# Seven products of quarters for the attention's values, in one stage behind the first gates

## The chip, the cores and the metric

The kernel runs on one core of a Trainium2 chip. The metric is the time of one execution on the device in microseconds (us); three executions of the kernel before gave a median of 658.37 us (658.17 to 658.61).

## The reference, cut to what matters

One layer of a hybrid encoder over 512 tokens of width 1024. A normed input `h` is projected once into ten groups of 1024 columns; two branches (attention with 8 heads of 128, retention with 4 heads of 256) are gated, projected and merged:

```
h = rms_norm(x, norm_gain)
sb_q, sb_k, sb_v, sb_g, r_q, r_k, r_v, r_g, m_sb, m_ret = split(h @ w_in)
z   = q.k / sqrt(128)                  # per head, 512 x 512, only s < t
w   = sigmoid(z) * prod_{s<j<t} (1 - sigmoid(z_j))
out_a = (w @ v) * silu(sb_g)
out_b = rms_norm(retention(r_q, r_k, r_v)) * silu(r_g)
merged = sigmoid(m_sb + b0) * (out_a @ w_a) + sigmoid(m_ret + b1) * (out_b @ w_b)
out = x + merged @ w_o
```

The change concerns `sb_v`, a product of 512x1024 by 1024x1024.

## The kernel before, in words

Every fp32 product is made of three matmuls of rounded parts (`mm3`: hi by hi, hi by lo, lo by hi). A weight block is loaded by SyncE (SP), rounded to `hi` by ScalarE (ACT) and its rest `lo` is taken by VectorE (DVE); that pair is `split`, line 131 its DVE half. A *stage* (`dense`) makes 512 columns: for eight row blocks k and four output blocks j it issues three matmuls, 96 in all. It holds four of five PSUM banks. The stages in order: `qk0`, `v0`, `sg0`, `qk1`, `qk2`, `v1`, `sg1`, `qk3`, `ma0`, `rqk0`, `pa0`, `ma1`, `pa1`, `rg0`, `rv`, and then the retention's and the last ones. `qk` makes queries and keys of two heads, `v` and `sg` values and gates of four heads, `ma` merge gates, `rqk` the retention's queries and keys, `pa` the attention's output projection.

The stage `rv` is of another kind: it makes the 1024 columns of the retention's values at once, by seven products of 256 tokens by 512 rows by 512 columns (Strassen) in place of eight (`v_groups`, `strassen`, `quarter_sums`). Its weights come as quarters (`w_rv`), and four sums of the tokens' quarters (`s1`, `s2`, `s3`, `n4`) are made ahead of it on GpSimd (POOL) and split (`token_sums`, `made_sums`).

Small work runs beside the stages: generators in a list (`Interleaver`), of which the first is resumed at each `work.step()`, after each second j of a row block, so sixteen times a stage. The instructions of a generator thus stand on TensorE (PE) between six matmuls of the stage and the next six. Side work is: the transposes of queries and keys (`post` in `qk_group`, which waits `W_QK` = 8 steps and makes `pqk`), the row copies of the norm (`token_norm_rows`: `rc` on DVE, `pr` on PE), and `attention` for two heads: `z` (scores), then `beta` (two sigmoids on ACT, on DVE the mask's add, a scan, a product), `pw` (transposes of beta on PE, then split into `wT`), `po` (weights by values), and `oa` (`po` by gates, split). Its order is one `z` block, then `pw` of two blocks earlier, and `po` when a head is done. TensorE's order is that of the code. Where a result is needed that the side list has not yet made, `drain` resumes the list with no stage's matmuls between: `pa0` does so at row block k for `oa[k]`, since row block k is head k:

```
    def branch_act(parts):
        def act(k):
            work.drain(lambda: k in parts)
            return parts[k]
```

The other engines' order is set by a scheduler that knows priorities (`tc.high_priority` around the weights' splits) and its own estimates; SP's loads stay in the order of the code.

Of the kernel before, what the change touches and what calls it, by code (L numbers as in the profile page):

```python
# [7 lines left out]
F32 = mybir.dt.float32  # L8
# [5 lines left out]
S = 512  # L14
# [55 lines left out]


@with_exitstack
def hybrid_block(ctx, tc, x, x_t, vecs, w_in, w_rv, w_a, w_b, w_o, cos_t, sin_t, decay, out):
    nc = tc.nc
    PSUM = bass.MemoryType.PSUM

# [28 lines left out]
    def T_tile(name, dtype=F32R):  # L105
        return big.tile([P, 4, S], dtype, tag="T", bufs=4, name=name)
# [54 lines left out]
    def first_loads():  # L161

        raws = [wpool.tile([P, 2, S], F32, tag="raw", bufs=RAW_BUFS, name=f"first_raw{k}") for k in range(2)]
        xt = [T_tile(f"xt{hf}", F32) for hf in range(2)]
        for k in range(NK):
            ks = slice(k * P, (k + 1) * P)
            if k < 4:
                load_weights(raws[k // 2][:, k % 2 : k % 2 + 1, :], w_in, k, 1, ((C_Q, 256), (C_K, 256)))
            load(xt[k // 4][:, k % 4, :], x_t[ks, :])
        for k in range(NK):  # L170
            r = xt[k // 4][:, k % 4, :]
            g = vec[:, V_NG + k : V_NG + k + 1]
            for c in range(0, S, S // 2 if k == 0 else S):
                cs = slice(c, c + (S // 2 if k == 0 else S))
                nc.scalar.activation(xT_hi[:, k, cs], r[:, cs], AF.Copy, scale=g)  # L175
            nc.vector.scalar_tensor_tensor(  # L176
                xT_lo[:, k, :], r, g, f32(xT_hi[:, k, :]), op0=ALU.mult, op1=ALU.subtract
            )
        return raws

    first = first_loads()

    idle = tmp.tile([P, 2 * S], mybir.dt.bfloat16, tag="tmp", name="idle")[:, :S]
    nc.vector.memset(idle, 0.0)
# [70 lines left out]
    def proj(name, blocks, rows):  # L255
        return dense(name, lambda k: (xT_hi[:, k, :], xT_lo[:, k, :]), w_in, blocks, rows)
# [5 lines left out]
    sr = const.tile([P, S], F32, name="sr")  # L262

    def token_norm():
        yield 9
        ssx = small.tile([P, NT], F32, tag="ssx", bufs=1, name="ssx")
        ts = []
        for hf in range(2):
            t = T_tile(f"x{hf}", F32).rearrange("p a s -> p (a s)").rearrange("p (b d) -> p b d", b=2)
            ts.append(t)  # L270
            load(t, x[2 * hf * P : (2 * hf + 2) * P, :].rearrange("(b p) d -> p b d", p=P))
        for hf, t in enumerate(ts):
            for j in range(2):
                tb = 2 * hf + j
                s2 = small.tile([P, 2], F32, tag="s2", name="s2")
                sq = tmp_tile("sqx")
                for c in range(2):
                    nc.scalar.activation(sq, t[:, j, c * S : (c + 1) * S], AF.Square, accum_out=s2[:, c : c + 1])
                nc.vector.tensor_add(ssx[:, tb : tb + 1], s2[:, 0:1], s2[:, 1:2])
        rsqrt(rx, ssx, D, NT)  # L280
        nc.gpsimd.tensor_mul(rx2, rx, rx)
        yield 1

    def token_norm_rows():

        load(cr, cos_t)
        load(sr, sin_t)
        yield 5
        pr = side_psum("pr")
        for tb in range(NT):  # L290
            rc = tmp_tile("rc")[:, :P]
            nc.vector.tensor_copy(rc, rx[:, tb : tb + 1].broadcast_to([P, P]))
            matmul(pr[:, tb * P : (tb + 1) * P], rc, ident, start=True, stop=True)
        nc.vector.tensor_copy(rb, pr)
        nc.gpsimd.tensor_mul(cr, cr, rb)
        nc.gpsimd.tensor_mul(sr, sr, rb)
        yield 1
# [3 lines left out]
    def qk_group(p):  # L301

        ps = proj(f"qk{p}", ((C_Q + 256 * p, 256), (C_K + 256 * p, 256)), True)
        ss = small.tile([P, NT, 4], F32, tag="ss", name=f"ss{p}")
        raws = []
        for tb in range(NT):
            raw = tmp.tile([P, 4, P], F32, tag="qraw", bufs=4, name=f"qraw{p}_{tb}")
            nc.scalar.copy(raw, ps[tb].rearrange("p (h d) -> p h d", h=4))
            raws.append(raw)
        for tb in range(NT):  # L310
            sq = tmp_tile("sqq").rearrange("p (h d) -> p h d", h=4)
            nc.scalar.activation(sq, raws[tb], AF.Square)
            nc.vector.reduce_sum(ss[:, tb, :], sq, axis=mybir.AxisListType.X)
        rr = small.tile([P, NT, 4], F32, tag="rr", name=f"rr{p}")
        nc.vector.tensor_mul(ss, ss, rx2.rearrange("p (b o) -> p b o", o=1).broadcast_to([P, NT, 4]))
        rsqrt(rr.rearrange("p b h -> p (b h)"), ss.rearrange("p b h -> p (b h)"), HD, 16)
        nc.gpsimd.tensor_mul(rr, rr, rx.rearrange("p (b o) -> p b o", o=1).broadcast_to([P, NT, 4]))
        for tb in range(NT):
            nc.gpsimd.tensor_tensor(
                raws[tb], raws[tb],  # L320
                rr[:, tb, :].rearrange("p (h o) -> p h o", o=1).broadcast_to([P, 4, P]), op=ALU.mult,
            )

        def post():
            hi, lo = T_tile(f"qk_hi{p}"), T_tile(f"qk_lo{p}")
            yield W_QK
            for tb in range(NT):
                pt = side_psum(f"pqk{p}_{tb}").rearrange("p (h d) -> p h d", h=4)
                for j in range(4):
                    transpose(pt[:, j, :], raws[tb][:, j, :], ident)  # L330
                ts = slice(tb * P, (tb + 1) * P)
                for c, a in ((V_QG, 0), (V_KG, 2)):
                    g = vec[:, c : c + 1]
                    nc.scalar.activation(hi[:, a : a + 2, ts], pt[:, a : a + 2, :], AF.Copy, scale=g)
                    nc.vector.scalar_tensor_tensor(
                        lo[:, a : a + 2, ts], pt[:, a : a + 2, :], g, f32(hi[:, a : a + 2, ts]),
                        op0=ALU.mult, op1=ALU.subtract,
                    )
# [7 lines left out]
    def v_group(name, c0):

        ps = proj(name, ((c0, S),), True)
        hi, lo = V_tile(f"{name}_hi"), V_tile(f"{name}_lo")
        for sb in range(NT):  # L350
            v_rows(hi, lo, sb, ps[sb])
        return [(hi[:, sb, :], lo[:, sb, :]) for sb in range(NT)]

    def v_rows(hi, lo, sb, src):
        r = rx[:, sb : sb + 1]
# [16 lines left out]
        split(hi, lo, t)  # L372
        sums[name] = (hi, lo)

    def token_sums(ready):

        xt = [V_tile(f"xs{hf}", F32) for hf in range(2)]
        for hf in range(2):
            load(xt[hf], x_t[4 * hf * P : 4 * (hf + 1) * P, :].rearrange("(k p) t -> p k t", p=P))
        yield 4  # L380
        for hf in range(2):
            for k in range(4):
                r = xt[hf][:, k, :]
                nc.scalar.activation(r, r, AF.Copy, scale=vec[:, V_NG + 4 * hf + k : V_NG + 4 * hf + k + 1])
                yield 1
        (x11, x21), (x12, x22) = halves(xt[0]), halves(xt[1])
        nc.gpsimd.tensor_sub(x22, x21, x22)
        nc.gpsimd.tensor_sub(x21, x11, x21)
        yield 1
        while not ready():  # L390
            yield 1
        made_sums("s1", x22)
        nc.gpsimd.tensor_sub(x22, x22, x11)
        yield 3
        made_sums("s3", x21)
        yield 3
        made_sums("s2", x22)
        nc.gpsimd.tensor_add(x12, x12, x22)
        yield 3
        made_sums("n4", x12)  # L400
        yield 1

    def quarter_sums(name, w, room):

# [82 lines left out]
        i, j = int(a[1]) - 1, int(a[2]) - 1  # L487
        return [t[:, 4 * j : 4 * j + 4, i * H : (i + 1) * H] for t in (xT_hi, xT_lo)]

    def v_groups(name, w):  # L490
        hi, lo = [V_tile(f"{name}0_hi")], [V_tile(f"{name}0_lo")]
        kept = {}

# [19 lines left out]
                elif n == 2:  # L513
                    v_rows(hi[0], lo[0], j, kept[1, j])

        room = [t(f"{name}_w{n}", F32) for n, t in enumerate((T_tile, V_tile, V_tile, T_tile))]
        strassen(name, w, room, put)
        hi.append(V_tile(f"{name}1_hi"))
        lo.append(V_tile(f"{name}1_lo"))
        for n in (3, 5):  # L520
# [187 lines left out]

    work.add(token_norm())
    qk_group(0)  # L710
    work.add(attention((0, 1), lambda: 0 in sg, lambda: v[0], lambda: sg[0]))
    v[0] = v_group("v0", C_V)
    sg[0] = silu_group("sg0", C_G)
    qk_group(1)
    work.add(attention((2, 3), lambda: 0 in sg, lambda: v[0], lambda: sg[0]))
    qk_group(2)
    work.add(attention((4, 5), lambda: 1 in sg, lambda: v[1], lambda: sg[1]))
    v[1] = v_group("v1", C_V + S)
    sg[1] = silu_group("sg1", C_G + S)
    qk_group(3)  # L720
    work.add(attention((6, 7), lambda: 1 in sg, lambda: v[1], lambda: sg[1]))
# [6 lines left out]
    for g in range(2):  # L728
        m = gate_group(f"ma{g}", C_MA + S * g, V_BM + 4 * g)
        if g == 0:  # L730
            ret(0, lambda: 5 in oa)
        else:
            work.side.insert(0, token_sums(lambda: len(pa) == 2))
            work.wait = 0
        ps = dense(f"pa{g}", branch_act(oa), w_a, ((S * g, S),), False)
        t = T_tile(f"pa{g}", F32)
# [114 lines left out]
```

## Time and profile before

| | before |
|---|---|
| median of three executions | 658.37 us |
| profiled execution, its own time | 658.81 us |
| its span (first to last instruction) | 657.0 us |
| TensorE busy | 650.5 us, 3073 matmuls |
| VectorE, ScalarE, GpSimd busy | 393.7, 276.2, 65.6 us |
| granted TensorE clock | full in all 40 slices |

The span is what the instructions cover; 1.8 us of the execution's own time lie around it. Matmuls are pipelined, so a matmul's shown duration (0.39 us for 512 columns) is longer than the distance from one to the next.

### The profile page before, as it was taken

The page shows a single profiled execution, that of the slowest core. Times are in us where ns is not written, and L with a number is a line of the kernel's source. Part 1 is how long each engine was busy: PE and PEld are TensorE (multiplying, and loading weights), DVE is VectorE, ACT ScalarE, POOL GpSimd, SP SyncE. Part 2 cuts the span into 40 slices and gives each one's busy share as a digit, 9 for nine tenths or more (in the row PEclk, how much of TensorE's full clock was granted, in tenths as well). Part 3 has the DMA queues.
Part 4 walks back from the last instruction along what each step waited for, and adds up shares of the span by engine and source line. Part 5 has one row for each costly group of instructions (what it writes and reads, how often), then busy time and mean ns, then how long its engine had stood idle before and what let it go on. Part 6 is the DMA issues. An engine that isn't in the chain of part 4 may idle for free.

```text
span 657.0 us, 7987 instructions
## 1 busy us (share of the span) xinstructions
PE 650.5 (99%) x3073; PEld 539.7 (82%) x3073; DVE 393.7 (60%) x582; ACT 276.2 (42%) x439; POOL 65.6 (10%) x58
## 2 busy tenths in 40 slices
PE   9999999999999999999999999999999999999997
PEld 6788888888888888888888878888888888888885
DVE  6356863596497477664464876386673862554632
ACT  5744534564364564332733554333342442422310
POOL 0051001250000400000330100200100101000000
PEclk9999999999999999999999999999999999999999
DMA  8543223322322312332538522232322322225441
GB/s 280 202 128 96 65 64 97 97 64 66 97 64 65 97 64 65 103 95 89 210 97 299 126 55 65 81 96 65 108 69 81 97 64 82 81 97 165 156 157 64
DMA packets 42503, 69.22 MB, mean 105 GB/s; under 512 B 2913, under 2 KB 19553, under 8 KB 42209
## 3 DMA queue, kind: packets, MB, share of 16 engines
q1 hardware_dynamic: 41168, 65.55, 31.4%
q0 software_dynamic: 576, 2.10, 1.7%
q10 hardware_dynamic: 720, 1.07, 0.4%
q8 instruction: 24, 0.39, 0.3%
q14 instruction: 15, 0.11, 0.1%
HBM read 65.55 MB, written 2.10 MB: 103 GB/s over the span
## 4 chain that ended last, share of the span: by engine, by line
PE 94%; DMA 3%; DVE 1%; ACT 1%; SPq 0%; issue 0%; DVEq 0%; ACTq 0%
PE rqk_ps L91 13%; PE qk_ps L91 10%; PE v_ps L91 7%; PE sg_ps L91 7%; PE pa_ps L91 7%; PE mb_ps L91 7%; PE ma_ps L91 7%; PE rg_ps L91 7%; PE fin_ps L91 7%; PE pb_ps L91 7%; PE rv_y L91 3%; PE rv_p L91 2%; PE po L91 2%; PE z L91 2%; PE rz L91 2%; PE ro L91 2%
## 5 line engine op out<-in xcount | busy, mean ns | idle before, releaser
L91 PE MATMUL rqk_ps<-xT_hi,rqk_hi 128*128 128x512 f32 x128 | 50.9, 397 | 0.0
L91 PE MATMUL qk_ps<-qk_hi,xT_hi 128*128 128x512 f32 x128 | 50.5, 402 | 0.0
L91 PE MATMUL rqk_ps<-xT_hi,rqk_lo 128*128 128x512 f32 x128 | 50.0, 391 | 0.0
L91 PE MATMUL rqk_ps<-xT_lo,rqk_hi 128*128 128x512 f32 x128 | 50.0, 391 | 0.0
L91 PE MATMUL qk_ps<-qk_hi,xT_lo 128*128 128x512 f32 x128 | 49.2, 392 | 0.2 <-DVE xT_lo L176 0.2
L91 PE MATMUL qk_ps<-qk_lo,xT_hi 128*128 128x512 f32 x128 | 49.0, 390 | 0.0
L91 PE MATMUL pa_ps<-oa,pa_hi 128*128 128x512 f32 x128 | 39.6, 390 | 0.0
L91 PE MATMUL pb_ps<-ob,pb_hi 128*128 128x512 f32 x128 | 39.4, 389 | 0.0
L569 DVE TENSOR_TENSOR_SCAN beta<-beta,zero 128x128 f32<-128x128 f32 (+3 forms) x32 | 26.9, 840 | 7.5 <-ACT beta L567 7.5
L91 PEld LDWEIGHTS qk_ps<-qk_hi,xT_lo 128*128 128x128 f32 x128 | 23.9, 188 | 5.8 <-DVE xT_lo L176 0.6
L91 PEld LDWEIGHTS rqk_ps<-xT_hi,rqk_lo 128*128 128x128 f32 x128 | 24.0, 188 | 5.2
L91 PEld LDWEIGHTS pa_ps<-oa,pa_hi 128*128 128x128 f32 x128 | 23.9, 188 | 5.3 <-ACT rk L620 0.4
L91 PEld LDWEIGHTS qk_ps<-qk_hi,xT_hi 128*128 128x128 f32 x128 | 24.0, 188 | 5.2 <-ACT xT_hi L175 0.8
L91 PEld LDWEIGHTS pb_ps<-ob,pb_hi 128*128 128x128 f32 x128 | 24.0, 188 | 5.0
L91 PEld LDWEIGHTS rqk_ps<-xT_hi,rqk_hi 128*128 128x128 f32 x128 | 24.1, 188 | 4.4
L91 PEld LDWEIGHTS rqk_ps<-xT_lo,rqk_hi 128*128 128x128 f32 x128 | 24.1, 188 | 4.2
L91 PEld LDWEIGHTS qk_ps<-qk_lo,xT_hi 128*128 128x128 f32 x128 | 24.1, 188 | 4.1
L205 POOL TENSOR_TENSOR rr<-ms,m_half 128x16 f32<-128x16 f32 x4 | 11.7, 2913 | 150.7 <-DVE ms L204 150.7
L91 PE MATMUL v_ps<-v_hi,xT_hi 128*128 128x512 f32 x64 | 26.1, 408 | 0.0
L131 DVE TENSOR_TENSOR qk_lo<-qk_raw,qk_hi 128x1024 fp32r<-128x1024 f32 x14 | 17.1, 1223 | 14.9 <-ACT qk_hi L130 14.9
L567 ACT ACTIVATE beta<-z 128x128 f32<-128x128 f32 (+3 forms) x32 | 14.0, 436 | 28.5 <-DVE z L564 28.2
L91 PE MATMUL sg_ps<-xT_hi,sg_hi 128*128 128x512 f32 x64 | 25.8, 404 | 0.0
(255 smaller groups left out, 1738.4 us busy)
## 6 DMA issues: line engine op xcount, KB each, us to landing
rqk_raw<-in_w_in SPq DMA_DIRECT2D x32, 256.0 KB, 3.0
qk_raw<-in_w_in SPq DMA_DIRECT2D x28, 256.0 KB, 3.0
v_raw<-in_w_in SPq DMA_DIRECT2D x8, 512.0 KB, 3.8
sg_raw<-in_w_in SPq DMA_DIRECT2D x8, 512.0 KB, 3.6
ma_raw<-in_w_in SPq DMA_DIRECT2D x8, 512.0 KB, 3.6
pa_raw<-in_w_a SPq DMA_DIRECT2D x8, 512.0 KB, 4.0
rg_raw<-in_w_in SPq DMA_DIRECT2D x8, 512.0 KB, 3.7
mb_raw<-in_w_in SPq DMA_DIRECT2D x8, 512.0 KB, 3.6
```

The source lines that it names most:

```text
L91: tc.keep_in_program_order(nc.tensor.matmul(*a, **k))
L131: nc.vector.tensor_sub(lo, src, f32(hi))
L205: nc.gpsimd.tensor_tensor(dst, t[:, :width], m_half[:, :width], op=ALU.pow)
L567: nc.scalar.activation(keep[:, :n], z[:, :n], AF.Sigmoid, scale=-sc)
L569: nc.vector.tensor_tensor_scan(keep[:, :n][:, ::-1], keep[:, :n][:, ::-1], zero.broadcast_to([P, n]), 1.0, op0=ALU.mult, op1=ALU.add,)
```

## The change

`sb_v` is now made as `rv` is, by seven products, in one stage `v` for both groups of heads; the stages `v0` and `v1` go. It stands behind `sg0`, and all four rounds of `attention` are added behind it. The tokens' sums for it are made from the first loads of x (kept in `first_xt`, scaled in place by eight `tensor_scalar_mul` on DVE, line 270 of the change), and `token_sums`, `token_norm_rows` and `post(0)` are side work of `sg0`, in this order. The norm's own loads of x go to V tiles. The diff, cut to its core:

```
+    def token_norm():
-        yield 9
+        yield 5
+        for hf in range(2):
+            yield 1
+            for k in range(4):
+                r = first_xt[hf][:, k, :]
+                nc.vector.tensor_scalar_mul(r, r, vec[:, V_NG + 4 * hf + k : V_NG + 4 * hf + k + 1])
+        yield 1
+        first_sums(first_xt)
+        yield 1
...
-            yield W_QK
+            yield W_QK if p else 1
...
+        if p == 0:
+            work.add(token_sums(first_xt))
+            work.add(token_norm_rows())
         work.add(post())
-        if p == 0:
-            work.add(token_norm_rows())
...
+    def first_sums(xt):
+        (x11, x21), (x12, x22) = halves(xt[0]), halves(xt[1])
+        nc.gpsimd.tensor_sub(x22, x21, x22)
+        nc.gpsimd.tensor_sub(x21, x11, x21)
+    def token_sums(xt, gap=2):
+        (x11, x21), (x12, x22) = halves(xt[0]), halves(xt[1])
+        made_sums("s1", x22)
+        nc.gpsimd.tensor_sub(x22, x22, x11)
+        yield gap
+        made_sums("s3", x21)
+        yield gap
+        made_sums("s2", x22)
+        nc.gpsimd.tensor_add(x12, x12, x22)
+        yield gap
+        made_sums("n4", x12)
+        yield 1
...
     work.add(token_norm())
     qk_group(0)
+    sg[0] = silu_group("sg0", C_G)
+    work.drain(lambda: "n4" in sums and 0 in qk_parts)
+    v[0], v[1] = v_groups("v", w_v, (V_tile, V_tile, T_tile, T_tile))
     work.add(attention((0, 1), lambda: 0 in sg, lambda: v[0], lambda: sg[0]))
-    v[0] = v_group("v0", C_V)
-    sg[0] = silu_group("sg0", C_G)
     qk_group(1)
     work.add(attention((2, 3), lambda: 0 in sg, lambda: v[0], lambda: sg[0]))
     qk_group(2)
     work.add(attention((4, 5), lambda: 1 in sg, lambda: v[1], lambda: sg[1]))
-    v[1] = v_group("v1", C_V + S)
     sg[1] = silu_group("sg1", C_G + S)
     qk_group(3)
     work.add(attention((6, 7), lambda: 1 in sg, lambda: v[1], lambda: sg[1]))
```

Where the change moves instructions is seen in the order of three places. First TensorE at the end of the last attention round (head 7: `z7_3` the scores' last block, `pw7_1` to `pw7_3` the transposes, `po7` weights by values). Before it stands in the stage `rqk0`, and six matmuls of that stage lie at each "...":

```order
L91 MATMUL z7_3_2360<-qk_hi3_1997,qk_lo3_1998 128x512
...
L94 MATMUL pw7_1_2376<-ident_131,beta7_1_2279 128x128 x2
...
L94 MATMUL pw7_2_2394<-ident_131,beta7_2_2308 128x128 x3
...
L94 MATMUL pw7_3_2406<-ident_131,beta7_3_2365 128x128 x4
...
L91 MATMUL po7_2419<-wT_0_76,v1_hi_1470 128x512
L91 MATMUL po7_2419<-wT_1_77,v1_hi_1470 128x512
```

In the change it stands in the stage `pa0`, the rows following one another with nothing between, except at "...", where the rest of `po7` is left out; the last row shown is the first matmul of row block 7:

```order
L91 MATMUL z7_3_2591<-qk_hi3_2200,qk_lo3_2201 128x512
L94 MATMUL pw7_1_2601<-ident_131,beta7_1_2511 128x128 x2
L94 MATMUL pw7_2_2606<-ident_131,beta7_2_2540 128x128 x3
L94 MATMUL pw7_3_2612<-ident_131,beta7_3_2596 128x128 x4
L91 MATMUL po7_2619<-wT_0_76,v1_hi_842 128x512
L91 MATMUL po7_2619<-wT_1_77,v1_hi_842 128x512
...
L91 MATMUL pa0_ps0_2365<-oa7_2634,pa0_hi6_2571 128x512 x2
```

The tail of head 7 has moved from `rqk0`, with stage matmuls in each gap, to the end of `pa0`, with none. Likewise `po6` stands directly ahead of the matmuls of row block 6, which read `oa6`.

Second, VectorE where the last attention round begins (`z6_0` its first block's masking, `beta6_0` the scan and product behind it). Before, that is at the end of `ma0` (`qk_lo3` are the transposed queries and keys):

```order
L131 TENSOR_TENSOR rqk0_lo0_2193<-rqk0_raw0_2189,rqk0_hi0_2192 128x1024
L335 SCALAR_TENSOR_TENSOR qk_lo3_1998<-pqk3_3_2104,vec_81,qk_hi3_1997 128x2x128
L564 TENSOR_TENSOR z6_0_2125<-z6_0_2125,neg_mask_136 128x128
L335 SCALAR_TENSOR_TENSOR qk_lo3_1998<-pqk3_3_2104,vec_81,qk_hi3_1997 128x2x128
L569 SCALAR_TENSOR_TENSOR beta6_0_2130<-beta6_0_2130,zero_78 128x128
L564 TENSOR_TENSOR z6_1_2141<-z6_1_2141,neg_mask_136 128x128
L573 TENSOR_TENSOR beta6_0_2130<-beta6_0_2130 128x127
```

In the change it is at the start of `pa0` (`rm`, `rk`, `rqk_lo0`: the rotation of the retention's first queries and keys, 16 instructions of 512 columns, of which the last six are shown):

```order
L636 TENSOR_TENSOR rm0_1_1_2352<-rk0_1_2334,sr_149 128x512
L637 TENSOR_TENSOR rm0_1_3_2354<-rk0_1_2334,cr_148 128x512
L131 TENSOR_TENSOR pa0_lo4_2497<-pa0_raw4_2494,pa0_hi4_2496 128x1024
L638 TENSOR_TENSOR rm0_1_0_2351<-rm0_1_0_2351,rm0_1_1_2352 128x512
L639 TENSOR_TENSOR rm0_1_2_2353<-rm0_1_2_2353,rm0_1_3_2354 128x512
L574 TENSOR_TENSOR z6_0_2381<-z6_0_2381,neg_mask_136 128x128
L131 TENSOR_TENSOR rqk_lo0_2332<-rm0_1_0_2351,rqk_hi0_2331 128x512
L131 TENSOR_TENSOR rqk_lo0_2332<-rm0_1_2_2353,rqk_hi0_2331 128x512
L579 SCALAR_TENSOR_TENSOR beta6_0_2386<-beta6_0_2386,zero_78 128x128
L574 TENSOR_TENSOR z6_1_2397<-z6_1_2397,neg_mask_136 128x128
L583 TENSOR_TENSOR beta6_0_2386<-beta6_0_2386 128x127
```

The masking and the scan of head 6 have moved behind the rotation and behind the split of `pa0`'s third weight block. On TensorE `z6_0` now stands behind the first six matmuls of `pa0`, and `pw6_0`, which reads `beta6_0`, behind its first 24 and `z6_0` to `z6_2`.

Third, VectorE where the row copies `rc` stand (`ss0`: the sums for the norm of queries and keys). Before, they are four in a row with small ones between, ahead of `v0`'s splits:

```order
L292 COPY rc_539<-rx_145 128x128
L315 TENSOR_TENSOR ss0_305<-ss0_305,rx2_146 128x16
L292 COPY rc_542<-rx_145 128x128
L204 TENSOR_SCALAR ms_328<-ss0_305 128x16
L292 COPY rc_545<-rx_145 128x128
L292 COPY rc_548<-rx_145 128x128
```

In the change three splits of token sums (`s3`, `s2`, `n4`), one of `sg0`'s weights, and the first split (`v_blo1`) and sum of the values' quarters stand between them:

```order
L300 COPY rc_443<-rx_145 128x128
L323 TENSOR_TENSOR ss0_315<-ss0_315,rx2_146 128x16
L131 TENSOR_TENSOR s3_lo_380<-xt0_88,s3_hi_379 128x1024
L204 TENSOR_SCALAR ms_338<-ss0_315 128x16
L131 TENSOR_TENSOR s2_lo_402<-xt1_89,s2_hi_401 128x1024
L131 TENSOR_TENSOR sg0_lo4_433<-sg0_raw4_430,sg0_hi4_432 128x1024
L131 TENSOR_TENSOR n4_lo_419<-xt1_89,n4_hi_418 128x1024
L131 TENSOR_TENSOR v_blo1_579<-v_w0_566,v_bhi1_578 128x1024
L300 COPY rc_446<-rx_145 128x128
L443 TENSOR_TENSOR v_w0_566<-v_w0_566,v_w1_567 128x1024
L300 COPY rc_449<-rx_145 128x128
L300 COPY rc_452<-rx_145 128x128
```

The last `rc`, which `pr` on TensorE reads, has moved behind work on the quarters' first loads. `pr` stands on TensorE behind the first 54 matmuls of `sg0` (before: behind its first 18).

## Rows read from the trace of the kernel before

**Rows 1.** The page's busy times of the engines.
```profile
PE 650.5 (99%) x3073; PEld 539.7 (82%) x3073; DVE 393.7 (60%) x582; ACT 276.2 (42%) x439; POOL 65.6 (10%) x58
```

**Rows 2.** Waits of TensorE: us in total, times, longest; the only one after 30 us.
```profile
PE rv_y L91 <- DVE rv_c L509: 0.7, 2, 0.4
```

**Rows 3.** The chain of waits: start us, us, what; its last stage, `rv`, `pr`.
```profile
55.98 0.89 PE pr L91 x8
...
365.62 5.44 PE rv_y L91 x24
...
404.95 1.37 PE rqk_ps L91 x6
...
609.30 43.53 PE fin_ps L91 x192
```

**Rows 4.** Groups of instructions: one of the three groups of the stages v0, v1.
```profile
L91 PE MATMUL v_ps<-v_hi,xT_hi 128*128 128x512 f32 x64 | 26.1, 408 | 0.0
```

**Rows 5.** Timeline of VectorE, start of the kernel: start us, us, engine, line, operation.
```profile
9.63 0.42 DVE L220 CAST qk_hi<-first_raw 128x512 fp32r<-128x512 f32 x1
9.97 0.74 DVE L176 SCALAR_TENSOR_TENSOR xT_lo<-xt,vec,xT_hi 128x512 fp32r<-128x512 f32 x1
...
11.23 3.39 DVE L176 SCALAR_TENSOR_TENSOR xT_lo<-xt,vec,xT_hi 128x512 fp32r<-128x512 f32 x5
15.35 1.23 DVE L131 TENSOR_TENSOR qk_lo<-qk_raw,qk_hi 128x1024 fp32r<-128x1024 f32 x1 [0.73 <-ACT qk_hi L130]
```

**Rows 6.** Timeline of TensorE, start of the kernel and the third weight block.
```profile
1.20 3.92 PE L91 MATMUL pi<-idle 128*128 128x512 bf16 x9 [1.20 <-DVE idle L184]
...
16.87 0.39 PE L91 MATMUL qk_ps<-qk_lo,xT_hi 128*128 128x512 f32 x1
```

**Rows 7.** Timeline of VectorE and GpSimd: first row copy, rx, a token sum.
```profile
33.35 0.22 DVE L292 COPY rc<-rx 128x128 f32<-128x128 f32 x1
...
28.54 1.03 POOL L205 TENSOR_TENSOR rx<-ms,m_half 128x4 f32<-128x4 f32 x1 [26.74 <-DVE ms L204]
...
323.98 3.27 POOL L388 TENSOR_TENSOR xs<-xs 128x1024 f32<-128x1024 f32 x1
```

**Rows 8.** Timeline of the DMA queue and ScalarE: rv's quarters, issue and first use.
```profile
347.35 2.90 SPq L134 DMA_DIRECT2D rv_w<-in_w_rv x6
...
352.13 1.05 ACT L130 CAST rv_bhi<-rv_w 128x1024 fp32r<-128x1024 f32 x1 [1.96 <-DMA rv_w<-in_w_rv]
```

**Rows 9.** VectorE around the first rotation: busy by stretch, and its timeline.
```profile
273.60:287.50 13.90, 13.90 (x62) 11.18 (x61) 13.20 (x20) 6.93 (x10) 0.00 (x0) 1.00 0.26 77
...
273.61 0.68 DVE L624 TENSOR_TENSOR rm<-rqk_ps,cr 128x512 f32<-128x512 f32 x1
274.21 0.68 DVE L625 TENSOR_TENSOR rm<-rqk_ps,sr 128x512 f32<-128x512 f32 x1
```

**Rows 10.** Timeline of head 7's last blocks on TensorE, VectorE, ScalarE; below, oa0.
```profile
264.02 0.39 PE L91 MATMUL z<-qk_hi,qk_lo 128*128 128x512 f32 x1
264.44 0.30 DVE L564 TENSOR_TENSOR z<-z,neg_mask 128x128 f32<-128x128 f32 x1 [1.27 <-PE z L91]
265.47 1.23 DVE L569 TENSOR_TENSOR_SCAN beta<-beta,zero 128x512 f32<-128x512 f32 x1 [0.72 <-ACT beta L567]
266.80 0.69 DVE L573 TENSOR_TENSOR beta<-beta 128x511 f32<-128x511 f32 x1
268.94 0.60 PE L94 MATMUL pw<-ident,beta 128*128 128x128 f32 x4
269.63 0.59 ACT L130 CAST wT<-pw 128x512 fp32r<-128x512 f32 x1 [1.35 <-PE pw L94]
270.25 0.69 DVE L131 TENSOR_TENSOR wT<-pw,wT 128x512 fp32r<-128x512 f32 x1 [0.82 <-ACT wT L130]
...
84.38 0.68 DVE L595 TENSOR_TENSOR oa<-po,sg 128x512 f32<-128x512 f32 x1
85.75 0.69 DVE L131 TENSOR_TENSOR oa<-oa,oa 128x512 fp32r<-128x512 f32 x1 [0.49 <-ACT oa L130]
```

More of the change, by code (lines that the diff above doesn't have):

```diff
@@ L72, in hybrid_block @@
 @with_exitstack
-def hybrid_block(ctx, tc, x, x_t, vecs, w_in, w_rv, w_a, w_b, w_o, cos_t, sin_t, decay, out):
+def hybrid_block(ctx, tc, x, x_t, vecs, w_in, w_v, w_rv, w_a, w_b, w_o, cos_t, sin_t, decay, out):
     nc = tc.nc
@@ L178, in first_loads @@
             )
-        return raws
-    first = first_loads()
+        return raws, xt
+    first, first_xt = first_loads()
     idle = tmp.tile([P, 2 * S], mybir.dt.bfloat16, tag="tmp", name="idle")[:, :S]
@@ L268, in token_norm @@
         for hf in range(2):
-            t = T_tile(f"x{hf}", F32).rearrange("p a s -> p (a s)").rearrange("p (b d) -> p b d", b=2)
+            t = V_tile(f"x{hf}", F32).rearrange("p a s -> p (a s)").rearrange("p (b d) -> p b d", b=2)
             ts.append(t)
@@ L287, in token_norm_rows @@
         load(sr, sin_t)
-        yield 5
+        yield 1
         pr = side_psum("pr")
@@ L340, in post @@
             qk_parts[p] = (hi, lo)
+        if p == 0:
+            work.add(token_sums(first_xt))
+            work.add(token_norm_rows())
         work.add(post())
-        if p == 0:
-            work.add(token_norm_rows())
[L346 to L352, printed above, removed]
     def v_rows(hi, lo, sb, src):
@@ L373, in made_sums, with second_sums @@
         sums[name] = (hi, lo)
-    def token_sums(ready):
+    def first_sums(xt):
[13 more added lines that the diff above has]
+        made_sums("n4", x12)
+        yield 1
+    def second_sums(ready):
         xt = [V_tile(f"xs{hf}", F32) for hf in range(2)]
@@ L385, in token_sums @@
                 yield 1
-        (x11, x21), (x12, x22) = halves(xt[0]), halves(xt[1])
-        nc.gpsimd.tensor_sub(x22, x21, x22)
-        nc.gpsimd.tensor_sub(x21, x11, x21)
+        first_sums(xt)
         yield 1
@@ L391, in token_sums @@
             yield 1
[L392 to L401, printed above, removed]
+        yield from token_sums(xt, 3)
     def quarter_sums(name, w, room):
@@ L488, in tokens, with v_groups @@
         return [t[:, 4 * j : 4 * j + 4, i * H : (i + 1) * H] for t in (xT_hi, xT_lo)]
-    def v_groups(name, w):
+    def v_groups(name, w, kinds):
         hi, lo = [V_tile(f"{name}0_hi")], [V_tile(f"{name}0_lo")]
@@ L514, in put @@
                     v_rows(hi[0], lo[0], j, kept[1, j])
-        room = [t(f"{name}_w{n}", F32) for n, t in enumerate((T_tile, V_tile, V_tile, T_tile))]
+        room = [t(f"{name}_w{n}", F32) for n, t in enumerate(kinds)]
         strassen(name, w, room, put)
+        sums.clear()
         hi.append(V_tile(f"{name}1_hi"))
@@ L732, in hybrid_block @@
         else:
-            work.side.insert(0, token_sums(lambda: len(pa) == 2))
+            work.side.insert(0, second_sums(lambda: len(pa) == 2))
             work.wait = 0
@@ L742, in hybrid_block @@
     work.drain(lambda: "n4" in sums)
-    rv[0], rv[1] = v_groups("rv", w_rv)
+    rv[0], rv[1] = v_groups("rv", w_rv, (T_tile, V_tile, V_tile, T_tile))
     ret(1)
@@ L834 @@
         "w_in": np.asarray(w_in).reshape(D, -1),
+        "w_v": quarters(np.asarray(w_in).reshape(D, -1)[:, C_V : C_V + D]),
         "w_rv": quarters(np.asarray(w_in).reshape(D, -1)[:, C_RV : C_RV + D]),
```

## The prediction

> **What bounds the kernel now.** I read the busy times first [rows 1]: TensorE is busy 99% of the span, nothing else over 60%. A busy TensorE need not be one at its pace, so next come its waits and the chain of waits. After the first 30 us there is one wait, in `rv`, of 0.7 us [rows 2], and the chain consists of TensorE's own stages, the last of which runs 192 matmuls in 43.53 us [rows 3]. That is 0.2267 us for a matmul of 512 columns, and I use it as the pace. So at every place something else hides below TensorE's stream, and time changes in two ways only: matmuls go, or TensorE finds an operand missing. Nearly all work of the other engines is covered because it stands between matmuls of a stage; the change takes stages away and packs the same side work into fewer of them, so the order of TensorE is what I read longest.
>
> **The change, part by part.**
>
> *Seven products in place of eight.* `v0` and `v1` are 3 groups of 64 matmuls [rows 4], 192 in all, 43.5 us at the pace. Seven products are 7 x 24 = 168 matmuls, 38.1 us at the pace. The same stage exists: `rv` goes from 365.62 to 404.95, 39.3 us [rows 3], the difference being mostly the waits of [rows 2], where a sum must be taken from a bank before the next product adds to it. The new stage has the same order of products, so I take 39.3: **-4.2 us** (bounds: -5.4 with no wait, -2.5 if ScalarE and VectorE, which also split queries and gates there, add as much again and more).
>
> *Scaling the first loads.* Eight L270 instructions go to VectorE; five stand ahead of the split of the third weight block of `qk0`. VectorE is packed there until 11.23 + 3.39 = 14.62, then waits 0.73 and does that split from 15.35 to 16.58; TensorE's matmul that reads it starts at 16.87 [rows 5, 6]. So 0.73 + 0.3 us are free. The trace has no such instruction of 512 columns. Bounds for each: 0.34 us from one start to the next, as behind the cast of 512 columns [rows 5], and 0.60, as between two-tensor ones [rows 9]; five are 1.7 to 3.0 us, so the split ends at 17.55 to 18.85 and TensorE waits 0.7 to 2.0 us, or a tenth more for the signal. I take the cast's price, since both read one tensor: **+0.8 us**. The Trainium skill, "VectorE: DVE Perf Modes", section "The perf-mode tier table", says that fp32 copies and tensor_scalar from SBUF run at twice the pace of tensor_tensor, with which the 0.42 of the cast against 0.68 of the others agrees; by the page the price is the cast's.
>
> *Token sums.* Four POOL subtractions and additions (up to 3.27 us each, [rows 7]) stand ahead of `rx`, which was made at 28.54; they start when the scaling is done (about 18.5), wait for `s1`'s split, and end near 30, so `rx` comes some 2 us late. That is before anything reads it except `rc`, and at the start of `sg0` I count nothing.
>
> *The row copies.* Before, `rc` is made from 33.35 and `pr` reads it at 55.98 [rows 7, 3], over 20 us of cover. In the change `pr` stands 54 matmuls (12.2 us) into `sg0`, which starts near 28.5, so TensorE comes to it at 40.8. The last `rc` stands behind five splits of 1.23 us, which VectorE takes as ScalarE rounds them, and behind the first sum of quarters. The quarters are loaded behind `sg0`'s last weights, issued near 33 when the raw buffers come free; `rv`'s first quarter was used 4.8 us after its issue [rows 8], here another load of its size is ahead, so it is there at 38.4 and its pair at 40.2. Then the split to 41.3, the sum to 42.6, the copies to 43.0. **+2.3 us** (0 if the loads come 3 us earlier, 4 if later).
>
> *Fewer steps for attention.* `v0` and `v1` no longer host side work, so each round begins a stage later, and the last, heads 6 and 7, falls into `pa0`. Three things follow.
>
> First, `pw2_0` and `pw4_0` now stand 24 matmuls behind a stage's end, where VectorE still does that stage's norm; I put them at 0.4 us each, **+0.8** (0 to 2).
>
> Second, `beta6_0` stands on VectorE behind the rotation. From its first instruction, some 1.5 us ahead of `pa0`, VectorE has 16 instructions at 0.60 (the distance of the two in [rows 9]), 9.6 us; two weight splits, 2.4; three halves of `qk_lo3`, near 1.5; mask, scan and product of short blocks, 1.2. That is 14.7, so `beta6_0` is there 13.2 us into `pa0`. That this stretch is full is seen before, where VectorE is busy 13.2 of the 13.9 us of the rotation [rows 9], and nothing waits for it. TensorE gets to `pw6_0` after 24 matmuls (5.44) and `z6_0` to `z6_2` (three matmuls each of 256, 256 and 384 columns, 1.2 by the columns): 6.6 us. **+6.5 us** (5 to 7.5).
>
> Third, the tail, where TensorE has nothing between. `pw7_3` waits for `beta7_3`: before, the product ended at 267.49, 3.24 us behind the end of `z`'s last slot (264.25) [rows 10]; two small transposes fill 0.25: 3.0. `po7` needs both halves of `wT`: from the start of `pw` (268.94) to 270.94 it is 2.0, with the signal 2.1, of which `pw` itself (0.35) and one matmul fill 0.6: 1.5. `oa`: from 84.38 to 86.44 product, rounding and rest take 2.06 [rows 10], with a signal at each end 2.4, of which one matmul fills 0.2: 2.2, and that twice, for `oa6` and `oa7`, since `pa0`'s row blocks 6 and 7 read them at once. **+8.9 us** (7.5 with every engine waiting ready, 11 if splits of 1.23 us stand in the way).
>
> *The clock.* The trace shows full clock in every slice and no pause of TensorE that could tell. But its first nine matmuls, out of idleness, take 3.92 us [rows 6], 0.435 each, the pace of the lower level (512 columns at 1.2 GHz) though the record reads full: 1.9 us more than at the pace. I count that once, behind the 6.5 us pause: **+1.9** (0, or 5.7 if three of the pauses do it). The Trainium skill, "TensorE: Matmul & The Clock Gate", section "HAM oscillation — how this bites in real kernels", says that pauses between matmul bursts send the clock back to half, and each burst starts cold; no run here shows it in mid-kernel yet.
>
> **Sum.** -4.2 + 0.8 + 2.3 + 0.8 + 6.5 + 8.9 + 1.9 = +17.0 us, on the profiled execution's own time 658.81 gives 675.8; that execution lies 0.44 above the median, so **675.4 us**. All low ends give +5 to +7, all high ends near +31; both ends at once are unlikely.
>
> **The rivals.**
>
> *Products win, pauses don't.* TensorE loses less than 4.2 us in all and the kernel ends at 653 to 657. This needs one mechanism: that TensorE runs later matmuls past a waiting one, so that row blocks 6 and 7 of `pa0` and `ma1` fill the pauses of the tail. Against it: in [rows 10] `po` and `oa` come in the order of the code, and [rows 2] has TensorE waiting in `rv` with other products behind. It decides if the tail is under 1 us and `pw6_0` waits under 2.
>
> *The tail alone.* VectorE's queue reaches `beta6_0` in time, since the rotation can begin earlier than I have it or ScalarE's roundings don't hold it. Then 6.5 and the clock's 1.9 go: 667. For it: before, the rotation stood behind `oa7`. Against it: VectorE's sum of 14.7 us holds without any wait in it.
>
> *The clock falls at more pauses.* The page's rule applied at the tail too, where `pw`, `po` and `oa` leave three pauses within 10 us: two more restarts at 1.9, 679; with the row copies late as well, 683. For it: the start of the kernel; against it: the pauses of the tail are 1.5 to 3 us, with matmuls between.
>
> *The change doesn't do what it says:* the stage `v` could cost as much as two `dense` ones; then 680. `rv`'s 39.3 speaks against it.
>
> **How the numbers follow.** Forecast 0.75 (670 to 680.5), the clock's rival 0.12, the tail alone 0.10, products win 0.02, the last 0.01. The predicted time is the forecast's. The range takes in the tail alone and most of the clock's: 667 to 684. Only *products win* is not slower: faster by over 0.2% (1.3 us, about what a measurement of this kernel can tell) 0.02, the same 0.01, slower 0.97.
>
> **What would show it.** Right: `v` lasts about 39 us; TensorE waits for a DVE product of `beta` once for 5 us or more and once for about 3, for `oa` twice for about 2, for `wT` once, all in `pa0`, which with its `z`, `pw` and `po` takes near 50 us; `pr` waits for `rc` near 41 us; a row of matmuls at 0.43 us and a granted clock below full behind the long pause. Wrong: if `pa0` shows no wait for `beta`, the main term falls; if the granted clock stays full, 1.9 us go; if `qk0` runs through the third block without a gap, the scaling was free.

## The result, and the profile after

The changed kernel takes **687.2 us** (median of 4 executions, 684.9 to 687.6), the kernel before 658.45 us on the same chip: 1.0432 times, 95% interval 1.0419 to 1.0445. It is slower by 28.7 us, where +17.0 was forecast, and 687.2 lies above the range.

TensorE is still the engine to read, but no longer always busy. The page's row answers [rows 1]:

```profile
PE 659.1 (96%) x3049; PEld 543.4 (79%) x3049; DVE 425.1 (62%) x612; ACT 285.9 (42%) x453; POOL 87.0 (13%) x66
```

There are 24 matmuls fewer, and yet TensorE counts 8.6 us more as busy, and 26.5 us of the span are not busy at all, where before it was 6.5. The second is pauses; the first is slow matmuls and the beginnings of the pauses, which the shown duration of a matmul covers. The chain answers [rows 3]: the seven products run from 59.89 to 99.23, 39.3 us, and the last stage has not changed.

```profile
59.89 5.44 PE v_y L91 x24
...
99.23 1.36 PE qk_ps L91 x6
...
638.41 43.53 PE fin_ps L91 x192
```

TensorE's waits, of which there was one after 30 us before [rows 2] (us in total, times, longest):

```profile
PE pw L94 <- DVE beta L583: 8.5, 2, 5.6
PE pa_ps L91 <- ACT oa L130: 2.9, 2, 1.4
PE po L91 <- DVE wT L131: 2.6, 2, 1.8
PE sg_ps L91 <- DVE sg_lo L131: 2.5, 1, 2.5
PE pr L91 <- DVE rc L300: 1.7, 2, 1.2
...
PE qk_ps L91 <- DVE qk_lo L131: 0.8, 1, 0.8
PE po L91 <- ACT wT L130: 0.7, 1, 0.7
```

The waits were expected except two: `sg_lo` (the first gates' first low part) and `po` for `wT`. What was not expected in its size stands in the stretches: after the window come its length, the busy time of TensorE, its weight loads, VectorE, ScalarE and GpSimd (each with its instructions), the granted clock as a share of full speed, the DMA share and GB/s.

```profile
28.00:36.00 8.00, 5.49 (x16) 3.79 (x16) 7.67 (x12) 7.80 (x14) 4.03 (x4) 0.79 0.34 88
36.00:188.00 152.00, 148.74 (x710) 122.72 (x709) 111.50 (x166) 76.05 (x132) 35.24 (x24) 1.00 0.33 96
188.00:197.00 9.00, 7.21 (x30) 5.96 (x30) 5.15 (x8) 1.81 (x4) 0.00 (x0) 0.81 0.19 60
...
271.00:284.00 13.00, 7.37 (x37) 5.94 (x36) 12.69 (x23) 6.54 (x13) 0.00 (x0) 0.90 0.15 42
284.00:300.00 16.00, 16.00 (x70) 13.19 (x71) 10.37 (x20) 6.45 (x16) 0.00 (x0) 0.87 0.00 0
300.00:310.00 10.00, 8.33 (x35) 6.33 (x33) 3.33 (x6) 1.21 (x4) 0.00 (x0) 0.83 0.00 0
310.00:328.00 18.00, 12.78 (x41) 9.71 (x41) 10.06 (x13) 4.79 (x8) 0.00 (x0) 0.72 0.32 103
328.00:680.00 352.00, 351.34 (x1646) 294.00 (x1646) 198.91 (x258) 131.58 (x174) 28.87 (x20) 1.00 0.36 109
```

The stretches below full clock have in them, or right ahead of them, one of the pauses of 1.4 to 5.6 us; the longest pause in the two with 1.00 is 1.2 us. TensorE's timeline at the longest pause shows what that is: ahead of it a matmul's successor starts after 0.23 us, behind it after 0.43 us (287.15 to 287.58), until about 288.5.

```profile
277.42 0.62 PE L91 MATMUL pa_ps<-oa,pa_hi 128*128 128x512 f32 x2
277.89 0.40 PE L91 MATMUL pa_ps<-oa,pa_lo 128*128 128x512 f32 x1
283.92 0.45 PE L94 MATMUL pw<-ident,beta 128*128 128x128 f32 x1 [5.63 <-DVE beta L583]
...
287.15 0.63 PE L91 MATMUL z<-qk_lo,qk_hi 128*128 128x512 f32 x1
287.58 0.63 PE L91 MATMUL z<-qk_hi,qk_lo 128*128 128x512 f32 x1
```

The cause of the unexpected wait at the first gates is seen on two engines. VectorE at the first gates' first split, then GpSimd with the token sums:

```profile
23.12 2.45 DVE L131 TENSOR_TENSOR s_lo<-xt,s_hi 128x1024 fp32r<-128x1024 f32 x1 [3.38 <-ACT s_hi L130]
...
28.37 3.21 DVE L131 TENSOR_TENSOR sg_lo<-sg_raw,sg_hi 128x1024 fp32r<-128x1024 f32 x1 [0.29 <-ACT sg_hi L130]
...
32.35 1.22 DVE L131 TENSOR_TENSOR sg_lo<-sg_raw,sg_hi 128x1024 fp32r<-128x1024 f32 x1
...
22.08 2.41 POOL L380 TENSOR_TENSOR xt<-xt 128x1024 f32<-128x1024 f32 x1
...
28.13 2.36 POOL L391 TENSOR_TENSOR xt<-xt 128x1024 f32<-128x1024 f32 x1
```

The same split takes 1.22 us when GpSimd runs no token sum and 3.21 when GpSimd runs one from 28.13 to 30.49. It ends 1.1 us behind the sum's end, about its own duration: it seems to stand still until then. The split of 2.45 in the first row, too, ends 1.1 us behind the end of a token sum (24.49). The Trainium skill, "SBUF — State Buffer", section "SBUF: two separate sides", says that a VectorE instruction with two SBUF inputs and a GpSimd instruction that reads SBUF take a shared pair of ports for a whole instruction, and that the one that comes second fully blocks; these rows agree.

And `po` waits for `wT` where a head now ends across a stage's end. VectorE there, at the end of `sg1`: six of the gates' eight products stand ahead of head 3's last two `wT`.

```profile
186.57 1.28 DVE L540 TENSOR_TENSOR sg<-sg_ps,rb 128x512 f32<-128x512 f32 x2
187.76 1.22 DVE L131 TENSOR_TENSOR qk_lo<-qk_raw,qk_hi 128x1024 fp32r<-128x1024 f32 x1
188.90 2.49 DVE L545 TENSOR_TENSOR sg<-sg,sg_s 128x512 f32<-128x512 f32 x4
191.31 1.15 DVE L131 TENSOR_TENSOR wT<-pw,wT 128x384 fp32r<-128x384 f32 x2
```

So the theory to test (A): the loss comes from the attention's rounds standing a stage too late, from the half clock behind the pauses that follow, and in a smaller part from the sums on GpSimd. The rival (B): the seven products with their splits and sums are themselves the cost.

### The profile page after: what moved, and what is told of

Read it like the earlier page. It is cut to its first block, busy times and chain, and to the rows that moved or that the text cites. A ratio compares the mean times of both kernels' runs of the same rounds, so it can differ in the third digit from the quotient of the medians.

```text
span 685.6 us, 8008 instructions
## 1 busy us (share of the span) xinstructions
PE 659.1 (96%) x3049; PEld 543.4 (79%) x3049; DVE 425.1 (62%) x612; ACT 285.9 (42%) x453; POOL 87.0 (13%) x66
## 3 DMA queue, kind: packets, MB, share of 16 engines
q1 hardware_dynamic: 39856, 65.55, 29.7%
## 4 chain that ended last, share of the span: by engine, by line
PE 88%; DVE 5%; issue 3%; ACT 2%; POOL 1%; DVEq 0%; ACTq 0%; POOLq 0%
PE rqk_ps L91 13%; PE qk_ps L91 8%; PE pa_ps L91 7%; PE ma_ps L91 6%; PE mb_ps L91 6%; PE rg_ps L91 6%; PE fin_ps L91 6%; PE pb_ps L91 6%; PE sg_ps L91 6%; PE po L91 3%; PE rv_y L91 2%; PE v_y L91 2%; PE rv_p L91 2%; PE v_p L91 2%; PE z L91 2%
## 5 line engine op out<-in xcount | busy, mean ns | idle before, releaser
L91 PE MATMUL pa_ps<-oa,pa_hi 128*128 128x512 f32 x128 | 43.7, 422 | 3.3 <-ACT oa L130 2.9
L579 DVE TENSOR_TENSOR_SCAN beta<-beta,zero 128x128 f32<-128x128 f32 (+3 forms) x32 | 27.7, 872 | 10.4 <-ACT beta L577 10.3
L131 DVE TENSOR_TENSOR rqk_lo<-rqk_raw,rqk_hi 128x1024 fp32r<-128x1024 f32 x16 | 19.5, 1222 | 14.3 <-ACT rqk_hi L130 14.2
L91 PE MATMUL sg_ps<-xT_hi,sg_lo 128*128 128x512 f32 x64 | 25.9, 405 | 2.5 <-DVE sg_lo L131 2.5
```

The costliest lines, as they stand in the source:

```text
L91: tc.keep_in_program_order(nc.tensor.matmul(*a, **k))
L131: nc.vector.tensor_sub(lo, src, f32(hi))
L579: nc.vector.tensor_tensor_scan(keep[:, :n][:, ::-1], keep[:, :n][:, ::-1], zero.broadcast_to([P, n]), 1.0, op0=ALU.mult, op1=ALU.add,)
```

## The experiments

All are edits of the changed kernel, except the last, and all times are medians. "Pauses" and "slow matmuls" below are sums over TensorE's timeline, of what the distance from one row to the next has beyond the pace: by the single pauses, and by matmuls at 0.43 instead of 0.23 us (512 columns).

**Two plain products at the same place.**

```
-    v[0], v[1] = v_groups("v", w_v, ...)
+    v[0] = v_group("v0", C_V)
+    v[1] = v_group("v1", C_V + S)
```

> The values as two plain products of 64 blocks at the same place as in the changed kernel (no quarters, no token sums, no scaling of the first loads; the computation is whole). Theory A (the loss comes from the attention's rounds being pushed one stage later, and from the half clock behind its pauses): the two plain products cost 4.2 us more than the seven, the missing token sums give back about 6 us at the start of the first gates, the pauses near 278 and 300 to 328 us stay: 681 to 688 us. Theory B (the seven products, their splits and the token sums are what costs): 658 to 666 us.

Measured 682.9 us (1.0367, 1.0349 to 1.0385). With no quarter, no sum and no scaling in it the kernel keeps most of the loss, 24.4 of 28.7 us, and the same waits:

```profile
PE pw L94 <- DVE beta L582: 8.7, 2, 5.9
...
PE po L91 <- DVE wT L131: 2.6, 2, 1.8
```

Theory B falls as the main cause. Since the plain products cost 4.2 us more than the seven and the whole is 4.3 faster, what the seven need ahead of them (sums, scaling, the later row copies) costs some 8.5 us, an estimate from these two numbers.

**Small matmuls in the pauses, first try.**

```
+    def fill(ps, n):
+        b = ident.bitcast(mybir.dt.bfloat16)
+        for _ in range(n):
+            matmul(ps[:, :256], b[:, :P], b, start=True, stop=True)
...
+            fill(pw.rearrange("p i t -> p (i t)"), {(6, 0): 44, (7, 3): 22}.get((h, b), 0))
```

> The changed kernel with small bf16 matmuls on the identity, whose results nobody reads, in eight of TensorE's pauses (20 of 0.11 us before the first gates' first low part, 8 and 14 before the values of heads 1 and 3, 44 before the transposes of head 6's first row block, 22 before those of head 7's last, 5 before head 7's values, 11 each before the out-projection's steps 6 and 7), always shorter than the pause. Theory A with the clock: the pauses stay as long as they were, and the matmuls at 0.43 us behind them go to 0.23: 8 to 10 us less, 676 to 680 us, granted clock 1.00 in 28 to 36 and 284 to 328 us. Rival (the matmuls behind a pause are slow for another reason, their operands): 685 to 690 us, with the 0.43 us still there.

Measured 682.9 us (680.2 to 686.5): a miss. The 44 matmuls ahead of head 6's transposes themselves waited 4.4 us for the buffer that they were written to, and so came behind the pause; at the first gates the pause moved to 42 to 46 us.

```profile
PE pw L91 <- ACT beta L588: 4.4, 1, 4.4
PE sg_ps L91 <- DVE sg_lo L136: 2.7, 2, 2.4
```

**Small matmuls in the pauses, to a free bank.**

```
+            if (h, b) == (6, 0):
+                fill(ps_mm.tile([P, S], F32, tag="mm", name="f"), 44)
```

> The changed kernel with small bf16 matmuls on the identity, whose results nobody reads, in seven of TensorE's pauses, as in the earlier run with such matmuls, but none at the first gates, and those ahead of head 6's first transposes go to a free bank, so that they need not wait for a buffer. Theory A with the clock: the slow matmuls from 184 us on (9.4 us in the changed kernel's profile) mostly go, the pauses stay as long as they were: 678 to 681 us. Rival (the matmuls behind a pause are slow for a reason other than the pause): 685 to 690 us.

Measured 679.4 us (678.5 to 679.5), 7.8 us less than the changed kernel. The stretches from 184 us on, which had 0.72 to 0.90, have full clock, and the one at the first gates, where nothing was put in, stays low:

```profile
28.00:36.00 8.00, 5.48 (x17) 3.80 (x16) 7.67 (x12) 7.80 (x14) 4.06 (x4) 0.80 0.35 88
...
188.00:200.00 12.00, 11.77 (x65) 9.66 (x64) 7.46 (x11) 3.48 (x6) 0.00 (x0) 1.00 0.17 48
...
270.00:284.00 14.00, 13.19 (x85) 11.04 (x84) 13.57 (x26) 7.54 (x16) 0.00 (x0) 1.00 0.13 37
284.00:300.00 16.00, 16.00 (x88) 13.49 (x87) 11.19 (x21) 5.58 (x14) 0.00 (x0) 1.00 0.01 1
300.00:310.00 10.00, 8.72 (x56) 6.64 (x53) 4.39 (x8) 3.33 (x8) 0.00 (x0) 1.00 0.40 131
310.00:328.00 18.00, 17.33 (x85) 14.11 (x85) 10.63 (x14) 4.47 (x6) 0.00 (x0) 1.00 0.21 62
```

Since only idle TensorE was given work that nobody reads, the 7.8 us are the price of the half clock: most of it slow matmuls, the rest pauses that end sooner because the `z`, `pw` and `po` inside them are faster.

**No additions on the tokens.**

```
-        first_sums(first_xt)
...
-        nc.gpsimd.tensor_sub(x22, x22, x11)
-        nc.gpsimd.tensor_add(x12, x12, x22)
```

(The last two stay where the retention's sums are made.)

> The changed kernel without GpSimd's four additions on the tokens of the first loads (the products then take the scaled parts themselves, so the values come out wrong); scaling and splits stay. Theory A: only the start gains: the first gates' first low part is not held (2.7 us and the slow matmuls behind it, 1.7 us), the four copies for the row of norms are shorter (about 1 us): 680 to 683 us. Theory B2 (the early token sums are the main loss): 670 us or less.

Measured 677.7 us (1.0295, 1.0277 to 1.0314), 9.5 us less, where theory A had 4 to 7: far from the whole. The split of [rows 5]'s kind is back at its own length, and its wait is gone:

```profile
26.50 1.23 DVE L131 TENSOR_TENSOR sg_lo<-sg_raw,sg_hi 128x1024 fp32r<-128x1024 f32 x1 [0.78 <-ACT sg_hi L130]
```

By the timeline the pauses before 60 us fall from 6.0 to 1.2 and the slow matmuls there by 1.6, 6.4 together. A further 1.7 is slow matmuls that in this execution did not follow the pause before head 3's values (0.3 us of them where the changed kernel's profile has 2.0, behind the same pause of 2.0 us), and the rest, about 1.5, slow matmuls that are missing in the tail. I take these two not to be the sums' doing; no run shows it.

**Heads 0 and 1 beside the seven products.**

```
+    work.add(attention((0, 1), lambda: 0 in v, ...))
     v[0], v[1] = v_groups("v", w_v, ...)
-    work.add(attention((0, 1), lambda: 0 in sg, ...))
...
-            if n[0] % 3 == 1:
+            if n[0] % 3 == 1 and name == "rv":
```

> The changed kernel with heads 0 and 1 started ahead of the seven products instead of behind them, so that six of their eight rounds run beside the products; to leave the rounds their buffers, the quarters' pieces use two pairs of buffers instead of three. Theory A: the attention stands as early as in the kernel before, the pauses near 278 and 300 to 328 us go or shrink to what the kernel before had: 660 to 668 us. Theory B (the products' splits and sums are the cost): the rounds' work on VectorE and ScalarE adds to theirs, the stage becomes longer than 39.4 us plus the rounds' matmuls (some 5 us), and the whole stays at 678 us or more.

Measured 677.7 us (1.0300, 1.0268 to 1.0332). Neither number: the tail shrinks, but two pauses arise inside the products, of 4.1 us for `beta0_0` at 62 and of 1.7 for `wT` at 77 (the longest of that row, 4.5, is at 278, in `pa0`).

```profile
PE z L91 <- DVE wT L131: 6.2, 2, 4.5
PE pw L94 <- DVE beta L583: 4.1, 1, 4.1
```

**The wait of the transposes counted from their group.** In the changed kernel the eight steps of `W_QK` begin when `post` comes to the head of the list, although its group has long been done where the list is behind.

```
+        made = work.steps
...
-            yield W_QK if p else 1
+            yield 1
+            while work.steps < made + (W_QK if p else 0):
+                yield 1
```

> The changed kernel with one rule of the side work changed: the transposes of a query-and-key group wait until eight steps after that group's own end, instead of eight steps after their turn in the queue comes (for group 0 nothing changes). Theory A (the rounds stand too late): where the queue is behind, up to seven steps of 1.4 us are saved at each of groups 1 to 3, head 6 and 7 end some 25 us earlier, the pauses near 278 and 300 to 328 us and the slow matmuls behind them (22 us in all) mostly go, the start's losses stay: 663 to 670 us. Rival (the rounds only move their waits, since VectorE is the limit where they are denser): 677 us or more.

Measured 664.0 us (1.0084, 1.0066 to 1.0102): 23.2 us less than the changed kernel, with the seven products untouched. No wait for `beta` or `oa` is left:

```profile
PE sg_ps L91 <- DVE sg_lo L131: 2.5, 1, 2.5
PE po L91 <- DVE wT L131: 1.4, 2, 0.8
```

**The same, with the additions on VectorE.**

```
+        e = nc.vector if xt is first_xt else nc.gpsimd
-        nc.gpsimd.tensor_sub(x22, x21, x22)
-        nc.gpsimd.tensor_sub(x21, x11, x21)
+        e.tensor_sub(x22, x21, x22)
+        e.tensor_sub(x21, x11, x21)
```

(and the other two likewise; `first_sums` moves from `token_norm` to the head of `token_sums`)

> As the run with the counted wait, and the four additions on the tokens of the first loads are made by VectorE instead of GpSimd, behind the first gates' first split instead of ahead of it. Theory A: the pauses at the first gates' first low part and at the row of norms (about 5 us, and the slow matmuls behind the first, 2 us) go: 5 to 8 us less than the run with the counted wait, 656 to 663 us. Rival (what holds VectorE there is its own queue, not GpSimd): no less than 2 us below that run.

Measured 657.3 us (0.9990, 0.9981 to 0.9999), 6.7 us less. One thing was not as I had written it: the scheduler put all four additions ahead of the first split, not behind it. VectorE does four more instructions of 1.22 us there and is still done sooner:

```profile
26.28 1.22 DVE L399 TENSOR_TENSOR xt<-xt 128x1024 f32<-128x1024 f32 x1
27.43 1.22 DVE L131 TENSOR_TENSOR sg_lo<-sg_raw,sg_hi 128x1024 fp32r<-128x1024 f32 x1
```

**The same, and head 0 beside the products.** The edit is that of heads 0 and 1 above, for head 0 alone.

> As the run before it, and head 0's four rounds run beside the seven products (pieces with two pairs of buffers). Theory A: if the rounds are already early enough, nothing more is to be had: 655 to 663 us, within 3 us of the run before it; the products' stage gets longer by the rounds' matmuls (3 to 4 us), which leave the later stages. Rival (VectorE in the products' stage is too full for rounds): pauses of 2 us or more in that stage and 3 us or more above the run before it.

Measured 667.7 us (1.0142, 1.0127 to 1.0157), 10.4 above the run without it: the rival's number. The pauses are at 58 and 74 us, and slow matmuls (4 us) follow them:

```profile
PE z L91 <- ACT beta L586: 4.3, 1, 4.3
PE pw L94 <- DVE beta L591: 3.3, 1, 3.3
```

**Three attempts at the rest, and a control.** The scalings written behind the first projection, at the head of `token_sums`:

```
-        yield 5
+        yield 9
...
+            for hf in range(2):
+                yield 1
+                for k in range(4):
+                    r = xt[hf][:, k, :]
+                    nc.vector.tensor_scalar_mul(r, r, ...)
...
-    work.drain(lambda: "n4" in sums and 0 in qk_parts)
+    work.drain(lambda: "n4" in sums)
```

> As the run with the counted wait and VectorE's additions, and the eight scalings of the first loads stand behind the first projection too, beside the first gates, with the four splits of the sums one step apart; the products start without waiting for group 0's transposes. Theory A: the pause of 1.0 us in the first projection goes, and the 1.3 us before group 0's transposes; nothing else moves: 654 to 656.5 us, below the kernel before. Rival (the work only moves its wait into the first gates or the products): 657 us or more.

Measured 658.2 us (1.0003, 0.9994 to 1.0011), no gain, as the rival had it. Half of the edit did not come to be: in VectorE's order the scheduler put the scalings (now L388) where they had been, ahead of the third split, so that the pause in the first projection stays. And the row copies are late again: `pr` waits 1.5 us.

```profile
15.31 1.27 DVE L388 TENSOR_SCALAR xt<-xt,vec 128x512 f32<-128x512 f32 x3
16.50 1.22 DVE L131 TENSOR_TENSOR qk_lo<-qk_raw,qk_hi 128x1024 fp32r<-128x1024 f32 x1
```

The attention's start beside the last of the seven products, with that edit and without it:

```
+            if name == "v" and n == 4:
+                work.add(attention((0, 1), lambda: 0 in v, ...))
```

> As the run with the later scalings, and the attention of heads 0 and 1 starts four steps earlier, beside the last of the seven products. Theory A: heads 1 and 5 then end inside a stage and not across its end, and the pauses of 1.1 and 0.7 us before their values (with the slow matmuls behind them, 2.5 us in all) go: 652 to 655 us. Rival: the first rounds collide with the values' scaling on VectorE and ScalarE at the end of the products, or other heads now end across a stage's end: 656 us or more.

> As the run with the counted wait and VectorE's additions (657.3 us), and only the attention's start four steps earlier, beside the last of the seven products. Theory A: 654.5 to 657 us. Rival: 658 us or more.

Measured 657.0 us (0.9984, 0.9975 to 0.9993) and **655.95 us** (0.9968, 0.9956 to 0.9980). The first is above the 652 to 655 expected, the second within its range. The pause before head 1's values goes in both, that before head 5's (0.7 us) stays. The second, the changed kernel with counted wait, VectorE's additions and early start, is the fastest of all, 2.2 us below the kernel before.

The counted wait in the kernel before:

> The kernel before with the counted wait alone. Theory A: its attention already ends before its out-projection needs it and TensorE has no pause there, so nothing is to be had: 657.5 to 659.5 us. Rival (the counted wait is worth something by itself, whatever the order): 655 us or less.

Measured 658.2 us (1.0000, 0.9991 to 1.0009): there it is worth nothing, as theory A has it.

## Why the prediction was wrong

The direction and most places were right; the size fell short by 11.7 us, and the range did not hold it. By the steps, forecast and then measured, as sums over TensorE's timeline (the profiled span grew by 28.6 us, from 657.0 to 685.6):

| step | forecast | measured |
|---|---|---|
| seven products | -4.2 | -4.2 (59.89 to 99.23) |
| scaling, ahead of the third split | +0.8 | +1.0 (five ahead of it, 0.40 each) |
| token sums at the first gates | 0 | +2.7 |
| `pr` for `rc`, near 41 us | +2.3 | +2.4, at 45 |
| heads ending at a stage's end | +0.8, `pw` | +3.0, `po` |
| `pw6_0` for `beta6_0` | +6.5 | +5.8 |
| tail | +8.9 | +9.1 |
| clock | +1.9 | +8.8, what is left of 28.6 |

**The step that failed is "I count that once".** The restart was known from the first nine matmuls, and I gave it to the one pause above 5 us. The granted clock fell six times instead: behind pauses of 2.0 us (188 to 197) and 2.5 us (28 to 36) as well, and three times in the tail, with full clock between (1.00 in 309 to 312 and in 319.2 to 322.2). Small matmuls in the pauses from 133 us on took 7.8 us away. In the rival on the clock, my argument against it ("1.5 to 3 us, with matmuls between") was wrong, and it held too few places: its 679 has three restarts. The section "HAM oscillation — how this bites in real kernels" of the Trainium skill's page "TensorE: Matmul & The Clock Gate", which I weighed and then used once, tells of bursts that each start cold behind a wait, and the stretches of the profile after agree. The waits of its example are longer than most of the pauses here, and that pauses of 2.0 and 2.5 us do the same it does not say; there the measurement decides.

**"At the start of `sg0` I count nothing" failed too.** I looked at when the sums would be done, not at whom they stop while they run: VectorE's split took 3.21 us instead of 1.22. Moving the sums to VectorE took off 6.7 us with all that follows. That is the sums' cost with the restart and the row copies in it; without the additions the changed kernel lost 9.5, of which 6.4 lie at its start.

**The heads at a stage's end** were the right thought at the wrong instruction: `pw2_0` and `pw4_0` did not wait; `po1` and `po3` did, at the other end of the head, because VectorE's stage-end work (1.3 and 2.5 us of gates' products at 3, reductions at 1) stands ahead of `wT`.

**The range left out what the terms allowed.** Added again, their low ends give +7.8 and their high ends +29.7, not +5 to +7 and near +31. The measured +28.7 is thus close to all high ends at once, which the prediction called unlikely, and the range ended 25.6 above the kernel before.

**The row copies' number was luck.** +2.3 was forecast and +2.4 came, but both sides of the difference were off by more than 4 us. TensorE came to `pr` at 45.2 and not 40.8, late by the pause and the slow matmuls at the first gates. The last copy was done at 47.9 and not 43.0: from the end of the quarters' split (43.0) VectorE needed 5.0 us for three copies and the sum, beside GpSimd's products for the queries and keys, a cost that the sum of the prediction does not have.

```profile
42.89 1.06 DVE L300 COPY rc<-rx 128x128 f32<-128x128 f32 x1
43.87 2.08 DVE L443 TENSOR_TENSOR v_w<-v_w,v_w 128x1024 f32<-128x1024 f32 x1
45.87 2.06 DVE L300 COPY rc<-rx 128x128 f32<-128x128 f32 x2
...
41.97 5.88 POOL L327 TENSOR_TENSOR qraw<-qraw,rr 128x512 f32<-128x512 f32 x4
```

A copy takes 0.22 us in [rows 7], and the same sum of quarters 1.22 at 55.70, with GpSimd idle. At these lengths the copies would have been done near 44.8 (an estimate), ahead of TensorE. So GpSimd seems to hold VectorE here as well.

**What was right.** The products' price held to 0.1 us, and with plain products in their place most of the loss stayed. `beta6_0` behind the rotation and the tail were each within 0.7 us, with the waits that the signs named, in `pa0`. That most of the loss is displacement, not work, is shown by the counted wait: one rule of the list changed and 23.2 us came back. By the timeline of its profiled execution, some 22 us of pauses and slow matmuls between 260 and 330 us went, and 3.2 at the end of `sg1`, for which 1.0 came at head 5.

**What stays open:** whether a pause near 2 to 3 us lets the clock fall differs between runs (below), and what decides it was not tried. The 8.8 us of the clock are what is left of the sum; small matmuls, which were not put in at the first gates, took 7.8 off.

## What to carry to other kernels

Work that hides beside a stage costs nothing only as long as there is a stage left to hide beside: when a change takes stages away, count the steps of the hidden work, and look for fixed waits in its list that are now paid in sequence; here they cost 23 us and the saved matmuls 4. Price each pause of TensorE with what the matmuls behind it lose, from the rows of a cold start, and price it for every pause, not for the longest alone. Before you hand work to an idle engine, see in the trace whom it stops while it runs. A term that comes out right is checked like one that does not: its two sides can be off together.

## What was not expected of the hardware

The granted clock does not follow from the length of the pause alone. With the same pause at the first gates (2.5 us) the changed kernel had 0.79 in 28 to 36, and the run with the counted wait full clock:

```profile
28.00:36.00 8.00, 5.47 (x24) 3.91 (x23) 7.26 (x9) 8.00 (x16) 5.04 (x4) 1.00 0.25 70
```

This is the profiled execution of that run, its fastest (662.1 us); the three others took 663.8 to 664.9 us at a mean clock of 0.995 to 0.997 instead of 0.999, so it seems to have fallen somewhere in them. With this goes that executions of kernels with such pauses spread more: 684.9 to 687.6 us for the changed kernel and 680.2 to 686.5 for the first try with small matmuls, against 678.5 to 679.5 for the second try and 657.5 to 659.0 over all executions of the kernel before.
